# A pad of 96 or 224 bytes at the left end of the on-chip memory, in a two-layer decoder trunk

## The chip, the cores and the metric

The kernel runs on one core of one Trainium2 chip. The metric is the device time of one execution in microseconds; lower is better. Before the change the median of three runs is 2179.43 us (2175.47 to 2182.7).

## The reference

The program is a decoder trunk with 1024 positions, width 1024 and two layers, all in float32. Layer 0 mixes tokens with latent attention (12 heads, causal), layer 1 with sliding-window attention (12 query heads, window 128). In both layers 4 more heads attend to a memory of 256 rows. A layer ends in an output projection and a squared-ReLU MLP of width 4096:

```python
for i in range(DEPTH):
    hn = rmsnorm(x, attn_norm_g[i])
    mix, q_cross = mla_mixer(hn, ...) if i % 2 == 0 else swa_mixer(hn, ...)
    cross = memory_cross_attention(q_cross, mem_n, w_mem_kv[i])
    x = x + jnp.concatenate([mix, cross], axis=-1) @ w_o[i]
    a = jax.nn.relu(rmsnorm(x, mlp_norm_g[i]) @ w_up[i])
    x = x + (a * a) @ w_down[i]
return rmsnorm(x, final_norm_g)
```

## The kernel before, in words

**Matmuls in three parts.** Every large operand is split into a high part (rounded to the matmul type float32r) and a low part, the rest. A product is then three matmuls: high times high, high times low, low times high. Each is a stationary operand of 128x128, loaded by a weight load, against a moving operand of 128x512. In the rows of the profile the moving operand stands first behind the arrow: `psu<-x,d` writes the accumulator `psu`, streams `x`, and has `d` loaded as weights.

**The MLP.** Both big products use Strassen's scheme with seven block products, in two stages. The *up* stage takes 16 steps of 256 columns, each with seven products of 4 x 3 = 12 matmuls (lines 1347 to 1349, accumulators psu and psv). The *down* stage takes 7 x 16 steps, each of 4 x 3 matmuls (lines 1638 to 1640, psy and psz).

```python
1346            for k in range(4):
1347                nc.tensor.matmul(ps, wh[:, k, :], xh[:, k, :], ...)
1348                nc.tensor.matmul(ps, wh[:, k, :], xl[:, k, :], ...)
1349                nc.tensor.matmul(ps, wl[:, k, :], xh[:, k, :], ...)
```

In the up stage ACT multiplies the incoming weights by the gain (line 1247), DVE sums them, and ACT and DVE split them (lines 99 and 100) four products ahead of the matmuls; the DMAs of the raw weights are issued two steps ahead, into `mr` for even steps and into `d` for odd ones. What the chip does first and next is the order of the code: each engine has one list, and the DMAs named here are issued by SP.

**Other stages with large matmuls.** The output projection (`wo_phase`, lines 108 to 110, accumulator pswo) goes over its columns in two halves; the first half reads its weights from `woq`, the second from `g`. The input projection of layer 1 (`feat_mm`, lines 108 to 110, accumulator psf) makes 12 blocks of 128 features, each 2 x 24 matmuls; the first 6 blocks have their weights in `wsh` and `wsl`, the last 6 in `wf`. The input projection of layer 0 is psin (lines 117 to 120). Attention has the accumulators pss, psx, pso (layer 0), psw and a second pswo of 384 columns (layer 1) and pscx (memory).

**Two stacks of tiles.** On-chip memory is 128 partitions; a tile has the same byte address in each. Pools are stacked from both ends: `side="left"` from the low end, `"right"` from the high end. At the low end lies the pool `const`, whose last tile is the pad `padl`; above it lies `quad`, and then whichever left pool the stage needs. At the high end lies the pad `padr`, and then the right pools. The pads are filled with zeros once and read by nobody.

```python
220    padl = const.tile([P, 24], F32, name="padl")
221    padr_p = pool("padr", "right")
222    padr = padr_p.tile([P, 24], F32, name="padr")
223    nc.gpsimd.memset(padl, 0.0)
```

Nearly all large tiles are whole multiples of 512 bytes in a row (a row of 512 columns is 2048 bytes, a weight slice of 128 columns is 512), so all slices in a pool begin at one and the same place within 512 bytes. The addresses in the built program give these places:

| pools | side | tiles as the profile names them | place within 512, before |
|---|---|---|---|
| quad | left | mqq, mqf, mr, xnh, woq, wf, fa, xhls | 256 |
| hb, kvp, kv1p, qcp, q1p | left | q and k of every third head of layer 0, v, kh and kl, q, qc, kmh and kml of layer 1 | 256 |
| pa | left | wih, wil (rows of 3712 bytes) | 256, 128, 0, 384 in turn |
| rest, xnp, ws (the MLP's and wo_phase's) | right | d, i, g; x; uh, ul, wsh, wsl | 384 |
| hb1, at | right | the other heads, ph, pl, vh | 384 |
| cp, wu | right | cTh, cTl, wkv, wkn, wqr | 128 |

`quad` begins at byte 19,200, which is 37 x 512 + 256. So a matmul that takes one operand from quad and the other from a right pool has them at two places that differ by 128 bytes; one with both operands on one side mostly has them at equal places. The matmuls of 512 columns of the first kind are: four of the seven products of every up step (mqq and mqf move, i, x and d are loaded), the first half of both output projections (woq), most of psf, and 96 matmuls at the end of layer 1's down stage (`psy<-mqq,x`).

Of the kernel before, what the change touches and what calls it, by code (L numbers as in the profile page):

```python
# [9 lines left out]
F32 = mybir.dt.float32  # L10
# [9 lines left out]
P = 128  # L20
# [35 lines left out]
def trunk(  # L56
# [12 lines left out]
    def pool(name, side="left", space=None, bufs=1):  # L69
        kw = {"reuse_waits": "tile"}  # L70
        if space is not None:
            kw["space"] = space
        return tc.alloc_tile_pool(name=name, bufs=bufs, side=side, **kw)

    const = pool("const")
# [141 lines left out]
    cosb = const.tile([P, NT, 16], F32, name="cosb")  # L217
    sinb = const.tile([P, NT, 16], F32, name="sinb")

    padl = const.tile([P, 24], F32, name="padl")  # L220
    padr_p = pool("padr", "right")
    padr = padr_p.tile([P, 24], F32, name="padr")
    nc.gpsimd.memset(padl, 0.0)
# [1756 lines left out]
```

## Time and profile before

| | |
|---|---|
| median of three runs | 2179.43 us |
| profiled execution: span from first to last instruction | 2179.5 us |
| TensorE matmul busy | 2133.9 us, 98% of the span, 10045 instructions |
| VectorE, ScalarE, GpSimd busy | 1489.4, 1149.7, 162.7 us |
| mean granted TensorE clock | 0.991 |

Consecutive matmuls overlap in the records: the next starts some 230 ns after one whose recorded time is some 390 ns. What a matmul costs in a dense stretch is therefore the distance from its start to the start of the next, which the timeline shows. A row of groups reads: line, engine, operation, output<-moving,weights, shape, count | busy us, mean ns of one | idle us before it. A row of windows reads: from:to, length, busy us (count) of PE, of PEld (weight loads), of DVE, ACT and POOL, then the granted clock, the busy share of the DMA engines and GB/s. A row of waits reads: who waited, for whom: us in total, times, longest us. A row of the chain reads: start us, us, what.

### The profile page before, as it was taken

Reading aid. Unit: us, or ns where it says so; the run is one execution under the profiler, and the core shown is the slowest. Engines: PE = TensorE matmul, PEld = TensorE weight load, DVE = VectorE, ACT = ScalarE, POOL = GpSimd, SP = SyncE. Lnnn points to the kernel's source line nnn. Section 1 sums busy time; section 2 is a strip of 40 time slices with the busy share of each in tenths; the row PEclk is TensorE's granted clock in tenths of the full one; section 3 lists DMA queues with packets and bytes.
Section 4 is the critical chain, followed back from the end, with each engine's and each line's share of the span. In section 5 each row is a group of like instructions: output and inputs, shape, how many; then the busy total and the mean of one; then the engine's idle time right before and its main releaser. Section 6 shows DMA issues by size and latency. Waiting matters only on the chain.

```text
span 2179.5 us, 29333 instructions
## 1 busy us (share of the span) xinstructions
PE 2133.9 (98%) x10045; PEld 1719.3 (79%) x10045; DVE 1489.4 (68%) x2845; ACT 1149.7 (53%) x2494; POOL 162.7 (7%) x226
## 2 busy tenths in 40 slices
PE   7999999999999999999999999999999999999998
PEld 6888677668788888788888778668888888888887
DVE  7566678765887776786657453665887776885665
ACT  5455477765754444444445453776755544444452
POOL 0012000001000000000001133440000000000000
PEclk9999999989999999999999999999999999999999
DMA  7202222323254445964533111113254445954442
GB/s 249 66 1 67 51 59 46 88 92 110 80 175 151 144 144 170 341 197 126 165 117 107 53 39 49 39 55 120 78 179 145 160 157 177 329 183 145 127 120 88
DMA packets 170948, 271.96 MB, mean 125 GB/s; under 512 B 15681, under 2 KB 71726, under 8 KB 170798
## 3 DMA queue, kind: packets, MB, share of 16 engines
q1 hardware_dynamic: 164228, 253.80, 36.3%
q0 software_dynamic: 4016, 13.12, 1.7%
q10 hardware_dynamic: 2554, 3.17, 0.4%
q8 instruction: 79, 1.29, 0.2%
q14 instruction: 71, 0.58, 0.1%
HBM read 180.65 MB, written 76.81 MB: 118 GB/s over the span
## 4 chain that ended last, share of the span: by engine, by line
PE 89%; DVE 4%; ACT 3%; DMA 2%; issue 1%; POOL 0%; DVEq 0%; ACTq 0%; POOLq 0%
PE psy L1640 5%; PE psy L1638 5%; PE psy L1639 5%; PE psu L1349 5%; PE psu L1347 5%; PE psu L1348 5%; PE pss L850 4%; PE psz L1640 4%; PE psz L1638 4%; PE psz L1639 4%; PE psv L1349 4%; PE psv L1348 4%; PE psv L1347 4%; PE pso L880 3%; PE pswo L110 3%; PE pswo L108 2%
## 5 line engine op out<-in xcount | busy, mean ns | idle before, releaser
L1247 ACT ACTIVATE mr<-mr,gcol 128x256 f32<-128x256 f32 (+1 forms) x160 | 67.4, 477 | 63.8 <-DMA mr<-in_mlp_w_up_dram 56.8
L1638 PE MATMUL psy<-g 128*128 128x512 f32 x256 | 99.9, 390 | 0.0
L1639 PE MATMUL psy<-g 128*128 128x512 f32 x256 | 99.6, 389 | 0.0
L1640 PE MATMUL psy<-g 128*128 128x512 f32 x256 | 99.4, 390 | 0.0
L99 ACT ACTIVATE g<-i 128x512 fp32r<-128x512 f32 x79 | 49.7, 629 | 93.3 <-PE psz L1639 46.2
L860 ACT ACTIVATE p<-pss 128x384 f32<-128x384 f32 (+3 forms) x144 | 69.5, 486 | 55.1 <-PE pss L850 51.7
L99 ACT ACTIVATE i<-mr 128x512 fp32r<-128x512 f32 x78 | 49.1, 630 | 84.9 <-PE psu L1348 21.7
L1247 ACT ACTIVATE d<-d,gcol 128x256 f32<-128x256 f32 x128 | 57.9, 499 | 62.0 <-DMA d<-in_mlp_w_up_dram 55.2
L100 DVE TENSOR_TENSOR g<-i,g 128x512 fp32r<-128x512 f32 x79 | 55.1, 698 | 47.0 <-ACT g L99 47.0
L99 ACT ACTIVATE uh<-i 128x512 fp32r<-128x512 f32 x66 | 41.6, 630 | 84.6 <-PE psy L1639 40.7
L731 DVE TENSOR_REDUCE m<-psx 128x1 f32<-128x1024 f32 (+7 forms) x96 | 71.9, 752 | 16.4 <-PE psx L730 16.0
L100 DVE TENSOR_TENSOR pl<-p,ph 128x512 fp32r<-128x512 f32 (+3 forms) x120 | 62.0, 526 | 30.4 <-ACT ph L99 29.1
L100 DVE TENSOR_TENSOR uh<-i,uh 128x512 fp32r<-128x512 f32 x66 | 45.5, 689 | 43.1 <-ACT uh L99 43.1
L1638 PE MATMUL psz<-g 128*128 128x512 f32 x192 | 74.7, 389 | 0.0
L1639 PE MATMUL psz<-g 128*128 128x512 f32 x192 | 74.7, 389 | 0.0
L1640 PE MATMUL psz<-g 128*128 128x512 f32 x192 | 74.7, 389 | 0.0
L100 DVE TENSOR_TENSOR i<-mr,i 128x512 fp32r<-128x512 f32 x78 | 53.6, 687 | 22.4 <-ACT i L99 22.4
L850 PE MATMUL pss<-ql,kh 97*128 97x384 f32 (+3 forms) x144 | 64.7, 449 | 0.0
L99 ACT ACTIVATE ph<-p 128x512 fp32r<-128x512 f32 (+3 forms) x120 | 59.5, 501 | 2.9
L1563 DVE TENSOR_TENSOR mqf<-mqq,mqf 128x512 f32<-128x512 f32 x64 | 43.1, 687 | 25.1 <-DMA mqq<-in_mlp_w_down_dram 24.9
L1640 PEld LDWEIGHTS psy<-g 128*128 128x128 f32 x256 | 48.0, 188 | 10.0
L1639 PEld LDWEIGHTS psy<-g 128*128 128x128 f32 x256 | 48.1, 188 | 9.9
(633 smaller groups left out, 7035.6 us busy)
## 6 DMA issues: line engine op xcount, KB each, us to landing
i<-hd SPq DMA_DIRECT2D x154, 256.0 KB
hd<-uh SPq DMA_DIRECT2D x76, 256.0 KB
hd<-ul SPq DMA_DIRECT2D x76, 256.0 KB
mr<-in_mlp_w_up_dram SPq DMA_DIRECT2D x36, 512.0 KB
hd<-x SPq DMA_DIRECT2D x72, 256.0 KB
mr<-hd SPq DMA_DIRECT2D x70, 256.0 KB
d<-in_mlp_w_up_dram SPq DMA_DIRECT2D x32, 512.0 KB
mqq<-in_mlp_w_down_dram SPq DMA_DIRECT2D x32, 512.0 KB
```

What stands on the lines that cost most here:

```text
L99: nc.scalar.activation(hi, src, AF.Copy)
L100: nc.vector.tensor_tensor(lo, src, f32(hi), ALU.subtract)
L731: return lambda: nc.vector.reduce_max(m8s[h][:, i : i + 1], ps[:, :n], axis=AX, negate=True)
L850: return lambda: nc.tensor.matmul(o, a, b, skip_group_check=True, **kw)
L860: nc.scalar.activation(p[:, c0:], ps, AF.Exp, scale=SC)
L1247: nc.scalar.activation(w[:, k, :], w[:, k, :], AF.Copy, scale=g_mlp[layer][:, k0 + k : k0 + k + 1])
L1347: nc.tensor.matmul(ps, wh[:, k, :], xh[:, k, :], start=p in (1, 2, 5) and k == 0, stop=False, skip_group_check=True)
L1348: nc.tensor.matmul(ps, wh[:, k, :], xl[:, k, :], start=False, stop=False, skip_group_check=True)
L1349: nc.tensor.matmul(ps, wl[:, k, :], xh[:, k, :], start=False, stop=k == 3, skip_group_check=True)
L1638: nc.tensor.matmul(ps, ah[:, j, :], bh, start=p in (1, 5, 2) and k == 0, stop=False, skip_group_check=True)
L1639: nc.tensor.matmul(ps, ah[:, j, :], bl, start=False, stop=False, skip_group_check=True)
L1640: nc.tensor.matmul(ps, al[:, j, :], bh, start=False, stop=k == NP - 1, skip_group_check=True)
```

## The change

One number changes:

```diff
-    padl = const.tile([P, 24], F32, name="padl")
+    padl = const.tile([P, 56], F32, name="padl")
```

The pad takes 224 bytes where it took 96. Every left tile above it moves up by 128 bytes: quad from 19,200 to 19,328, which is 37 x 512 + 384. The places within 512 become 384 for quad, hb, kvp, kv1p, qcp and q1p, and 384, 256, 128, 0 in turn for pa. The other tiles of const and all right tiles stay where they were.

The lists of instructions of PE, DVE, ACT and SP are the same before and after. On POOL one row differs, at the start of the program, where the pads are filled (`ident` is the identity, `eps_t` a constant):

```order
 L124 MEMSET ident 128x128
 L138 MEMSET eps_t 128x1
-L223 MEMSET padl 128x24
+L223 MEMSET padl 128x56
 L224 MEMSET padr 128x24
 L143 DMA sinks_b<-in_swa_sinks_dram 128x12
```

Nothing moved: the filling of the pad has 32 columns more, and what follows stands in the same order.

## The prediction

> **What bounds the kernel now.** I read the page first, for its busy shares and the chain that ended last.
>
> ```profile
> span 2179.5 us, 29333 instructions
> PE 2133.9 (98%) x10045; PEld 1719.3 (79%) x10045; DVE 1489.4 (68%) x2845; ACT 1149.7 (53%) x2494; POOL 162.7 (7%) x226
> PE 89%; DVE 4%; ACT 3%; DMA 2%; issue 1%; POOL 0%; DVEq 0%; ACTq 0%; POOLq 0%
> ```
>
> The chain runs through PE for 89% of the span. Since a recorded matmul overlaps the next one, a busy PE may still be slow, so the windows by stage come next: the first half of layer 0's output projection, its up stage, one up step, a piece of its down stage, the wf blocks of layer 1's input projection, and layer 1's up stage.
>
> ```profile
> 485.00:530.00 45.00, 44.34 (x192) 35.30 (x191) 30.12 (x41) 27.10 (x60) 3.85 (x7) 1.00 0.47 156
> 606.00:894.00 288.00, 287.99 (x1250) 234.21 (x1250) 208.34 (x328) 138.70 (x279) 1.90 (x1) 1.00 0.51 171
> 642.62:661.99 19.37, 19.37 (x86) 15.77 (x84) 14.14 (x23) 9.51 (x19) 0.00 (x0) 1.00 0.44 146
> 950.00:1050.00 100.00, 100.00 (x442) 82.78 (x442) 67.52 (x109) 42.69 (x74) 0.00 (x0) 1.00 0.47 145
> 1309.00:1375.00 66.00, 66.00 (x285) 53.12 (x284) 23.43 (x31) 21.31 (x32) 18.02 (x41) 1.00 0.14 41
> 1575.00:1866.00 291.00, 291.00 (x1264) 237.08 (x1263) 214.75 (x340) 142.18 (x284) 0.00 (x0) 1.00 0.51 171
> ```
>
> In the up and wf stages PE has no idle time at all, with the clock granted in full (1.00). So their time is the number of matmuls times the distance between two starts, and anything that shortens that distance is worth all of it. In one up step of 19.37 us DVE is busy for 14.14 and ACT for 9.51 us; neither becomes the bound if the step shrinks by a third of a microsecond.
>
> Is the distance the same for all matmuls? The groups by form say no. First the four kinds of product in the up stage and one of the down stage, all 128x512 with the same three-part scheme:
>
> ```profile
> L1348 PE MATMUL psv<-mqq,i 128*128 128x512 f32 x112 | 44.2, 395 | 0.0
> L1348 PE MATMUL psv<-mqf,x 128*128 128x512 f32 x112 | 44.2, 395 | 0.0
> L1348 PE MATMUL psv<-g,d 128*128 128x512 f32 x112 | 43.6, 389 | 0.0
> L1348 PE MATMUL psu<-x,d 128*128 128x512 f32 x128 | 49.8, 389 | 0.0
> L1639 PE MATMUL psy<-g 128*128 128x512 f32 x256 | 99.6, 389 | 0.0
> ```
>
> The two that stream a quad tile (place 256) against right weights (place 384) take 395 ns, the three with both operands at 384 take 389. They alternate within one step of 19 us, beside the same work of the other engines. The timeline of PE in the step from 642.62 gives the distance: 48 matmuls of the first kind up to 653.81, then 36 of the second up to the next step.
>
> ```profile
> 642.62 0.40 PE L1347 MATMUL psu<-mqq,i 128*128 128x512 f32 x1
> ...
> 653.81 0.39 PE L1347 MATMUL psu<-g,i 128*128 128x512 f32 x1
> ...
> 661.99 0.40 PE L1347 MATMUL psu<-mqq,i 128*128 128x512 f32 x1
> ```
>
> That is 11.19 / 48 = 233.1 ns each, against 8.18 / 36 = 227.2 ns. A longer stretch of equal places, 78 distances in the down stage, fixes the pace that I expect after the change:
>
> ```profile
> 1000.14 0.39 PE L1638 MATMUL psy<-g 128*128 128x512 f32 x1
> ...
> 1017.82 0.39 PE L1638 MATMUL psy<-g 128*128 128x512 f32 x1
> ```
>
> 17.68 / 78 = 226.7 ns.
>
> **The change part by part.** The longer filling of the pad is one POOL instruction ahead of the first matmul's inputs, 32 columns more; POOL is busy 7% of the span and the chain gives it 0%: nothing. All the rest is places: quad moves from 256 to 384, where the right tiles are.
>
> *Up stages.* 48 of the 84 matmuls of a step go from 11.19 us to 48 x 226.7 ns = 10.88 us: 0.31 us a step. 16 steps in two layers: 32 x 0.31 = 9.9 us. By the recorded durations (395 against 389) it is 1536 x 6 ns = 9.2 us; I take 9.9, since the distance is what adds up.
>
> *Output projections.* The first halves read weights from woq, the second halves from g:
>
> ```profile
> L109 PE MATMUL pswo<-woq,x 128*128 128x512 f32 x64 | 25.3, 395 | 0.0
> L109 PE MATMUL pswo<-woq,d 128*128 128x512 f32 x64 | 25.3, 395 | 0.0
> L109 PE MATMUL pswo<-g,d 128*128 128x512 f32 x112 | 43.6, 390 | 0.0
> ```
>
> Each of the two upper rows is one of three lines in one layer: 2 x 192 = 384 matmuls at 5 ns, 1.9 us. Here PE does idle a little (44.34 busy of 45.00 us), so between 0 and 1.9; I take 1.9, because PE is busy for 98% of that window.
>
> *Input projection of layer 1, wf blocks.* Both xnh and wf are in quad, x is on the right, so one matmul in three has unequal places; yet all three are slow:
>
> ```profile
> L108 PE MATMUL psf<-xnh,wf 128*128 128x512 f32 x96 | 38.1, 397 | 0.0
> L109 PE MATMUL psf<-x,wf 128*128 128x512 f32 x96 | 37.9, 395 | 0.0
> L110 PE MATMUL psf<-xnh,wf 128*128 128x512 f32 x96 | 37.7, 392 | 0.0
> 1310.10 0.40 PE L108 MATMUL psf<-xnh,wf 128*128 128x512 f32 x1
> ...
> 1312.20 0.40 PE L108 MATMUL psf<-xnh,wf 128*128 128x512 f32 x1
> ```
>
> Nine distances take 2.10 us, 233.3 ns each. After the change all three kinds are at 384, which is the state of the down stage: 288 x (233.3 - 226.7) = 1.9 us. That a matmul at equal places pays here for its neighbours means the price belongs to the stream, not to one pair.
>
> *The wsh blocks.* Weights on the right, two of three moving operands in quad. Fifteen distances:
>
> ```profile
> 1300.00 0.39 PE L109 MATMUL psf<-x,wsh 128*128 128x512 f32 x1
> ...
> 1303.43 0.39 PE L109 MATMUL psf<-x,wsh 128*128 128x512 f32 x1
> ```
>
> 3.43 / 15 = 228.7 ns: 288 x 2.0 = 0.6 us.
>
> *End of layer 1.* 96 matmuls with xnh's old tiles:
>
> ```profile
> L1639 PE MATMUL psy<-mqq,x 128*128 128x512 f32 x32 | 12.6, 395 | 0.0
> ```
>
> 96 x 6 = 0.6 us.
>
> *Layer 0's input projection and attention.* wih's rows go round through all four places against weights in quad; both shift alike, so their relative places stay, and I take 0. If the absolute place counted, 192 matmuls could gain 5 ns (1.0 us):
>
> ```profile
> L118 PE MATMUL psin<-wil,xhls 128*128 128x512 f32 x64 | 25.2, 394 | 0.0
> ```
>
> Attention has its operands at equal places on one side already: 0.
>
> *DMAs into left tiles.* These now end at places that are odd multiples of 128, as the right ones always did. The up weights land in both kinds of tile in turn, mr on the left, d on the right:
>
> ```profile
> ACT mr L1247 <- DMA mr<-in_mlp_w_up_dram: 56.8, 27, 3.1
> ACT d L1247 <- DMA d<-in_mlp_w_up_dram: 55.2, 24, 3.4
> ```
>
> A wait is 56.8 / 27 = 2.1 us for the left and 55.2 / 24 = 2.3 us for the right, 9% more at most. In the up stage PE covers that. It isn't covered where the chain itself stands on a load into a left tile:
>
> ```profile
> 37.07 4.88 DMA fa<-in_mla_w_in_dram
> 44.29 3.23 DMA fa<-in_mla_w_in_dram
> 430.61 3.96 DMA wor<-in_w_o_dram
> 886.71 7.64 DMA mqf<-in_mlp_w_down_dram
> ```
>
> These are 19.71 us; 9% is 1.8 us. Between 0 and 1.8 I take half, +0.9. The Trainium skill ("DMA: Bandwidth & Descriptors", How a descriptor splits into AXI transactions) speaks against the change here: a transaction must start at a multiple of 256 bytes, so a piece that starts elsewhere costs an extra, partly unused one. By it a 1 KB piece would need 36 beats for 32, an estimate of 12.5% or 2.5 us in place of 0.9; the trace's 9% in waits neither excludes it nor needs it.
>
> Sum: 9.9 + 1.9 + 1.9 + 0.6 + 0.6 = 14.9 us gained, less 0.9: 14.0. The profiled execution has a span of 2179.5 us, the median of the runs is 2179.43, so no correction: 2179.5 - 14.0 = **2165.5 us**, 0.64% less.
>
> **The rivals.** A change of over 0.3% (6.5 us) is what a measurement of this kernel can tell from none.
>
> *The left side is slow wherever its tiles begin: 2179.5 us.* Every slow row above has a quad operand, so side and place are confounded in the MLP. Two rows part them, a matmul of 256 columns with both operands on the left at 256, and one of 384 with both on the right at 128:
>
> ```profile
> L379 PE MATMUL pscx<-kml,qc 128*128 128x256 f32 x64 | 15.9, 282 | 0.0
> L120 PE MATMUL psv<-wkvh,cTl 128*128 128x384 f32 x32 | 8.5, 335 | 0.0
> ```
>
> On the right, 128 columns fewer cost 389 - 335 = 54 ns less, so 256 columns should take 335 - 54 = 281. The left takes 282. A left side that is slow by itself would have added some 3 to 6 ns. The wf rows keep this rival alive: there even left with left is slow. Chance 0.10. The Trainium skill ("TensorE: Matmul & The Clock Gate", Part 2, on the weight load) would have it so too: the moving operand and the weight load have two independent read ports, and a load takes no bandwidth from the running matmul. By that rule places could not matter; the alternation of 395 and 389 within a step is not explained by it.
>
> *Only part of it goes: about 2172.5 us.* If a part of the price hangs on something else that tells quad from the rest, half of the 14.0 us comes. Nothing in the rows gives a half, except that wsh blocks with two unequal pairs in three pay only 2.0 ns. Chance 0.05.
>
> *Equal places collide on the left: 2183.9 us.* The slowest row of all, 397 ns, is a pair with both operands in quad at the same place. If that is what equal places do as soon as a quad tile is in the pair, the 1536 + 384 + 192 + 96 = 2208 matmuls of the terms above (192 of the wsh blocks) go from 395 to 397: 2208 x 2 ns = 4.4 us more. It decides if the up products come out above 395. Against it: the same line's sister, L110, has equal places too and takes 392, and all right-right rows stand at 389. Chance 0.03.
>
> **How the numbers follow.** My forecast has 0.82. By itself it reaches from 2179.5 - 14.9 - 1.0 = 2163.6 (no DMA price, psin gains) to 2179.5 - 14.9 + 1.9 + 1.8 = 2168.3 (no gain in the output projections, the whole DMA price). The runs shown lie from 4.0 below to 3.3 above their median, and the forecast stands on one execution, so I add that and a little for terms that I took at 0 (4.6 below, 5.7 above): 2159 to 2174. That holds the forecast and most of the half case, and leaves out under 2 in 10. Faster by over 0.3%: nearly all of the forecast and half of the half case, 0.84. Within 0.3%: the first rival, the rest of the half case, part of the collision, 0.13. Slower by more: 0.03, the collision with the DMA price on top.
>
> **What would show it.** Right: the rows psu and psv <- mqq and mqf fall from 395 to 389 and an up step from 19.37 to 19.05 us; the three wf rows become one number near 389; the rows of g and of attention stand still; in the up windows PE stays at 100%. The DMA term is right if waits for mr come near those for d. Wrong: mqq and mqf rows still at 395 (the side, not the place), between 390 and 394 (part of it), above 395 (a collision); or the rows fall and the span doesn't, in which case PE idles in the up windows and ACT or a DMA is what it waits for.

## The result

| | median us | runs | against the kernel before |
|---|---|---|---|
| before | 2180.88 | 13 (2175.47 to 2183.93) | |
| changed | 2174.58 | 13 (2171.13 to 2179.19) | 0.9973, 95% interval 0.9963 to 0.9983 |

The change is worth 6.3 us, 0.27%. The forecast was 14.0 us. So the kernel is faster, by less than half of what was expected.

### The profile page after: what moved, and what is told of

Same layout as the page of the kernel before. It is cut to its first block, busy times and chain, and to the rows that moved or that the text cites. A ratio compares the mean times of both kernels' runs of the same rounds, so it can differ in the third digit from the quotient of the medians.

```text
span 2169.4 us, 29333 instructions
## 1 busy us (share of the span) xinstructions
PE 2118.5 (98%) x10045; PEld 1714.9 (79%) x10045; DVE 1488.9 (69%) x2845; ACT 1147.7 (53%) x2494; POOL 161.2 (7%) x226
## 3 DMA queue, kind: packets, MB, share of 16 engines
q1 hardware_dynamic: 164228, 253.80, 37.2%
## 4 chain that ended last, share of the span: by engine, by line
PE 84%; DVE 5%; DMA 4%; ACT 4%; issue 1%; POOL 0%; SPq 0%; DVEq 0%; ACTq 0%; POOLq 0%
PE psy L1638 5%; PE psy L1640 5%; PE psy L1639 5%; PE psu L1347 4%; PE psu L1349 4%; PE psu L1348 4%; PE psz L1638 4%; PE psz L1640 4%; PE psz L1639 4%; PE pss L850 4%; PE pso L880 3%; PE psv L1349 3%; PE psv L1348 3%; PE psv L1347 3%; PE pswo L110 2%; PE pswo L108 2%
```

## The profile after

The page of the changed kernel first: its span, its engines and the chain that ended last.

```profile
span 2169.4 us, 29333 instructions
PE 2118.5 (98%) x10045; PEld 1714.9 (79%) x10045; DVE 1488.9 (69%) x2845; ACT 1147.7 (53%) x2494; POOL 161.2 (7%) x226
PE 84%; DVE 5%; DMA 4%; ACT 4%; issue 1%; POOL 0%; SPq 0%; DVEq 0%; ACTq 0%; POOLq 0%
```

PE is busy for 15.4 us less (2133.9 before), of which some 5.5 us aren't the pad's work, as shown below. The chain stands on PE for 84% instead of 89%; DMA and ACT have grown in it. The groups by form after, the row of product 7 first:

```profile
L1347 PE MATMUL psu<-g,i 128*128 128x512 f32 x120 | 48.9, 408 | 3.6 <-ACT d L1386 2.0 <-ACT i L1386 1.4
L1348 PE MATMUL psv<-mqq,i 128*128 128x512 f32 x112 | 43.6, 389 | 0.0
L1348 PE MATMUL psv<-mqf,x 128*128 128x512 f32 x112 | 43.6, 389 | 0.0
L1348 PE MATMUL psv<-g,d 128*128 128x512 f32 x112 | 43.6, 389 | 0.0
L108 PE MATMUL psf<-xnh,wf 128*128 128x512 f32 x96 | 37.3, 389 | 0.0
L109 PE MATMUL psf<-x,wf 128*128 128x512 f32 x96 | 37.3, 389 | 0.0
L110 PE MATMUL psf<-xnh,wf 128*128 128x512 f32 x96 | 37.3, 389 | 0.0
L109 PE MATMUL pswo<-woq,x 128*128 128x512 f32 x64 | 24.9, 390 | 0.0
```

Before, the first of them was:

```profile
L1347 PE MATMUL psu<-g,i 128*128 128x512 f32 x120 | 47.0, 391 | 0.0
```

The slow rows shown have come down to 389 or 390 (395 before for mqq, mqf and woq; 397, 395 and 392 for wf), and the row of g with d stands still. The rows of wsh and wsl have not (405, 397 and 397 ns after, 407, 396 and 398 before), although their distances became a little shorter. The timeline of PE in the step that the prediction looked at (it began at 642.62 before) gives the distances:

```profile
635.18 0.39 PE L1347 MATMUL psu<-mqq,i 128*128 128x512 f32 x1
...
646.06 0.39 PE L1347 MATMUL psu<-g,i 128*128 128x512 f32 x1
...
654.22 0.39 PE L1347 MATMUL psu<-mqq,i 128*128 128x512 f32 x1
```

10.88 us for 48 matmuls and 8.16 for 36: 226.7 ns each in both, 19.04 us for the step (19.37 before). So far this is the forecast, to a hundredth of a microsecond. What is new is the first line of product 7, with 408 ns and 3.6 us of idle time (before: 391 and none). The windows show where it goes: the two up windows of the prediction, moved to the same matmuls, and inside the first the step above and the next one (second and third row).

```profile
598.55:887.25 288.70, 285.55 (x1251) 233.65 (x1251) 209.23 (x330) 138.31 (x279) 1.90 (x1) 1.00 0.51 170
635.18:654.22 19.04, 19.04 (x85) 15.77 (x84) 13.99 (x23) 9.37 (x19) 0.00 (x0) 1.00 0.46 149
654.22:674.17 19.95, 19.34 (x85) 15.69 (x84) 13.95 (x23) 9.33 (x19) 0.00 (x0) 1.00 0.41 135
1565.50:1855.20 289.70, 289.19 (x1265) 236.22 (x1264) 212.70 (x339) 140.97 (x284) 0.00 (x0) 1.00 0.52 171
```

The first step is as forecast. The next takes 19.95 us, more than the 19.37 of before, with PE idle for 0.61. The whole window takes 288.70 us where it took 288.00, and that of layer 1 took 291.00 and now 289.70: nearly all of the 9.9 us that the matmuls should save in the up stages is handed back there.

The timeline of the late step, PE first, shows one matmul that starts 1.00 us after the one before it:

```profile
664.88 0.39 PE L1349 MATMUL psv<-mqf,x 128*128 128x512 f32 x1
665.88 0.50 PE L1347 MATMUL psu<-g,i 128*128 128x512 f32 x1 [0.61 <-ACT d L1386]
```

It is the first of product 7. Products 6 and 7 both write `psu`, so product 7 must wait until ACT has copied product 6 out of it (line 1386). ACT in the same microseconds:

```profile
659.64 0.63 ACT L99 ACTIVATE i<-d 128x512 fp32r<-128x512 f32 x1 [1.03 <-PE psv L1348]
663.92 0.91 ACT L1247 ACTIVATE mr<-mr,gcol 128x256 f32<-128x256 f32 x2 [3.65 <-DMA mr<-in_mlp_w_up_dram]
664.73 0.61 ACT L99 ACTIVATE x<-d 128x512 fp32r<-128x512 f32 x1
665.25 0.57 ACT L1386 ACTIVATE d<-psu 128x512 f32<-128x512 f32 x1
```

ACT stood still for 3.65 us, waiting for the second half of a later step's raw weights; the gain of that half (line 1247) stands on ACT's list ahead of the copy that PE needs. The same place before the change:

```profile
671.00 0.91 ACT L1247 ACTIVATE mr<-mr,gcol 128x256 f32<-128x256 f32 x2 [2.82 <-DMA mr<-in_mlp_w_up_dram]
671.81 0.62 ACT L99 ACTIVATE x<-d 128x512 fp32r<-128x512 f32 x1
672.34 0.57 ACT L1386 ACTIVATE d<-psu 128x512 f32<-128x512 f32 x1
```

The same order, the same wait, but the copy ended at 672.91 and product 7 started at 673.22: some 0.3 us to spare in this step. After, product 7 is due 0.31 us earlier in the step, and the copy ends 0.68 us later in it (11.60 us after the step's start, 10.92 before). The load took most of that: from its issue to the start of its gain there are 5.27 us, and 4.66 before. The list of waits after:

```profile
ACT mr L1247 <- DMA mr<-in_mlp_w_up_dram: 75.1, 31, 3.8
ACT d L1247 <- DMA d<-in_mlp_w_up_dram: 67.9, 23, 4.2
...
PE psu L1347 <- ACT d L1386: 2.0, 3, 1.1
```

ACT waits for weights 143.0 us where it waited 112.0. The idle time that PE records is only part of the loss (0.61 us at the step above, where the start came 0.77 late). Summed over all distances between starts in the up stages that are longer than 300 ns, less 227 ns for each, PE loses 9.0 us after and 1.2 before: 7.8 more. Product 7 has 7.5 of the 9.0, and 0.3 of the 1.2.

The step shown is not like all others. From the end of the copy to the start of product 7, the 28 steps that follow the first two of each layer had between 0.05 and 1.94 us before, most of those of layer 1 0.9 to 1.2. After, 16 of the 28 have 0.05, which means that PE starts as soon as the copy is done. So the copies lost more than the 0.31 us by which product 7 came earlier, and the traces show two things that go with it:

- The second half is issued later in PE's step: 4.2 us after the step's start before and 4.9 after (means of ten steps of layer 1; 4.5 and 4.9 in layer 0).
- Four steps of layer 0 (4, 7, 10 and 13, counted from 0) lose 4.2 of the 7.5 us. In these the last packet of the load landed 3.9 to 4.7 us after the issue, where the median of all second halves is 3.5 to 3.6. In each of the four a packet of 16 KB ran beside the load for 1.05 to 1.57 us, on the queue that the profile names `instruction`; 9 to 27 of the load's 512 packets landed later than 3.6 us, the others did not. Before, steps 4, 7 and 10 have such a packet too, of 0.9 to 1.0 us, and landings of 3.9 to 4.2 us; in step 13 it came when the load had all but landed. That this packet is the cause was not tested. The row of that queue, with its packets, its MB and their share of the 16 engines' time:

```profile
q8 instruction: 79, 1.29, 0.3%
```

The two profiled executions differ by 10.1 us, the medians by 6.3. Part of that is the granted clock: in the attention of layer 0 it was 0.50 for 13.65 us before.

```profile
462.26:475.91 13.65, 13.65 (x32) 7.63 (x31) 3.86 (x7) 4.18 (x9) 0.00 (x0) 0.50 0.05 10
```

After the change the same stretch ran at full clock:

```profile
461.70:469.80 8.10, 8.10 (x34) 4.66 (x33) 3.76 (x6) 4.79 (x10) 0.00 (x0) 1.00 0.00 0
```

These 13.65 - 8.10 = 5.5 us are no work of the pad. The other way, a stretch at 0.50 in the attention of layer 1 was 3.4 us longer after (6.83 against 3.41), where PE lost 1.4 us.

## The experiments

The theory: the matmuls bring the 14.9 us of the prediction's sum everywhere, and some 8 of them are handed back in the up stages, because ACT's copy of product 6 is late behind a gain that waits for a DMA. The rivals: DMAs into left tiles are slower at their new place (A); something else than the weights is late (B). Since the up stages hold the whole question, this table has for every kernel the time from the first matmul of step 2 to the first of step 15, for both layers together (26 steps, read from the timelines of PE), and the long distances as counted above. Each interval is against runs of the kernel before that were taken beside it, whose medians were 2180.4 to 2181.3 us. By the prediction the 26 steps should go from 503.8 to 503.8 - 26 x 0.31 = 495.7 us.

| kernel | places left, right | median us | ratio to before, 95% interval | 26 up steps, us | long distances, us |
|---|---|---|---|---|---|
| before | 256, 384 | 2180.9 | | 503.8 | 1.2 |
| changed | 384, 384 | 2174.6 | 0.9963 to 0.9983 | 503.6 | 9.0 |
| changed, loads by POOL | 384, 384 | 2188.4 | 1.0020 to 1.0049 | 520.1 | 26.1 |
| before, loads by POOL | 256, 384 | 2191.3 | 1.0029 to 1.0061 | 518.3 | 17.2 |
| both at 256 | 256, 256 | 2168.9 | 0.9925 to 0.9964 | 499.0 | 4.4 |
| left at 320 | 320, 384 | 2184.6 | 1.0002 to 1.0025 | 506.3 | 3.3 |
| changed, copy by DVE | 384, 384 | 2164.8 | 0.9921 to 0.9957 | 495.9 | 3.3 |
| before, copy by DVE | 256, 384 | 2179.1 | 0.9982 to 1.0011 | 503.6 | 1.1 |
| changed, writes by POOL | 384, 384 | 2170.0 | 0.9941 to 0.9977 | 498.7 | 5.0 |
| both at 256, copy by DVE | 256, 256 | 2165.4 | 0.9923 to 0.9955 | 495.3 | 2.2 |
| both at 320 | 320, 320 | 2173.4 | 0.9956 to 0.9983 | 504.4 | 9.9 |
| 256 apart | 192, 448 | 2175.0 | 0.9968 to 0.9988 | 504.2 | 10.4 |

### Earlier loads, a failed attempt

```diff
-                nc.sync.dma_start(out=r[h], in_=...)
+                (nc.gpsimd if h and i > 2 else nc.sync).dma_start(out=r[h], in_=...)
```

On the changed kernel:

> The changed kernel, with the loads of the second half of each step's up weights (from step 3 on) issued by POOL instead of SP, so that they no longer stand behind SP's writes of the last results. Theory: the shorter distance (226.7 instead of 233.3 ns) is worth some 15 us on PE everywhere, and the up stages hand back 7.8 us because PE at product 7 (psu<-g,i) waits for ACT's evacuation of product 6, which is queued on ACT behind the gain of a half that has not landed. With the loads some 1.5 us earlier the wait at product 7 goes (under 2 us in place of 5.6 in the rows L1386), and the time is 2174.6 - 7 = about 2167. Rival A, loads into left tiles are slower at their new place: the waits of ACT's gain for mr stay longer than in the kernel before, and of the 7.8 us little comes back, 2172 to 2175. Rival B, something else than the weights (DVE's sums, the evacuations themselves) is late: PE's idle time at product 7 stays, 2174 to 2176.

And on the kernel before:

> The same edit of the loads on the kernel before (pad of 96 bytes), the control for the run above. Theory: PE had no idle time in the up stages of the kernel before, its step being 0.3 us longer, so earlier loads are worth at most 1.2 us there: 2179.5 to 2181. The pad is then worth 13 to 14 us between this pair, against 6.3 without the edit. Rivals A and B: the edit is worth as much or as little with either pad, so the pair stays 6 to 7 us apart.

Measured: 2188.4 and 2191.3 us. Both expectations fell, because the edit did the reverse of what it was chosen for. The list of DMA issues of the first of the two gives, for the loads that POOL issued:

```profile
d<-in_mlp_w_up_dram POOLq DMA_DIRECT2D x14, 512.0 KB, 5.2
mr<-in_mlp_w_up_dram POOLq DMA_DIRECT2D x12, 512.0 KB, 5.2
```

SP's issues have no such number in the list. Counted alike, from the issue of a second half to the start of its gain where ACT waited for it, the medians are 5.2 us when POOL issues and 4.0 when SP does (kernels before and after). So the pair is a test with later weights. As such it speaks for the theory: PE's wait at product 7 grows

```profile
L1347 PE MATMUL psu<-g,i 128*128 128x512 f32 x120 | 49.9, 416 | 16.5 <-ACT d L1386 8.3 <-ACT i L1386 8.1
```

from 3.6 to 16.5 us, still behind ACT's line 1386, and with both kernels waiting for weights the pad is worth only 2.9 us.

### Product 6's copy by DVE: the deciding run

```diff
-                nc.scalar.activation(s, ps, AF.Copy)
+                V.tensor_copy(s, ps) if p == 6 and i > 1 else nc.scalar.activation(s, ps, AF.Copy)
```

> The changed kernel, with product 6's copy out of its accumulator made by DVE instead of ACT from step 2 on (28 copies of 128x512), so that it no longer stands on ACT's list behind the gain that waits for the weights; loads, places and PE's list stay. Theory: PE's wait at product 7 for this copy (9.0 us of long distances in the up stages, 1.2 in the kernel before) falls to 3 us or less, and the time is 2174.6 - 6 = about 2168.5 (2167 to 2171). The loads still land as late as before (ACT still waits some 140 us for them), so a gain here shows that it is the place of the copy on ACT's list that costs, not the load by itself. Rival B, DVE is late as well (it is busy 14 of 19 us of a step): the wait at product 7 becomes one for DVE of the same size, 2173 to 2176. Rival E, the weights themselves are late for product 2 or 6 of the next step: PE's idle time moves there, 2173 to 2176.

Its control, with the pad of before:

> The same edit on the kernel before (pad of 96 bytes), the control of the run above. Theory: there is hardly anything to take away (1.2 us of long distances), and DVE has 28 copies more to do: 2179.5 to 2182. The pad is then worth 12 to 14 us between this pair, nearly the 14.9 of the matmuls. If the edit helps by as much here as there, the copy on ACT's list is a cost of its own and not what the pad's gain ran into: 2174 to 2176.

Measured: 2164.8 and 2179.1 us. The same edit is worth 9.8 us with the long pad, and 1.4 with the short one against the runs beside it (2180.5), where the interval holds no change. Between this pair the pad is worth 14.3 us by the medians. The rows of the changed kernel with this edit, groups and waits:

```profile
L1347 PE MATMUL psu<-g,i 128*128 128x512 f32 x120 | 46.7, 389 | 0.0
```

```profile
ACT mr L1247 <- DMA mr<-in_mlp_w_up_dram: 71.3, 31, 3.6
ACT d L1247 <- DMA d<-in_mlp_w_up_dram: 59.5, 23, 4.3
```

Product 7 doesn't wait any more (the 3.3 us of long distances that are left stand elsewhere, the largest, 1.0 us, in the last step of layer 1), although ACT still waits for weights for 130.8 us. So the late landing costs nothing by itself; what costs is that the copy stands behind it. The second halves are issued 4.3 us after the step's start in layer 1 here, as early as before the change, though the step is as short as in the changed kernel. So the later issue (4.9 us) came with the wait and not from the shorter step; through which link is not shown. The windows over the 26 steps:

```profile
621.84:869.52 247.68, 247.68 (x1092) 205.12 (x1093) 192.16 (x301) 112.28 (x226) 1.90 (x1) 1.00 0.49 161
1586.67:1834.93 248.26, 247.99 (x1094) 204.84 (x1093) 193.48 (x304) 113.45 (x227) 0.00 (x0) 1.00 0.49 162
```

247.68 / 13 = 19.05 us a step in layer 0, the number of the prediction, and 19.10 in layer 1. Rival B falls: DVE has the copies in addition (192.16 us busy of 247.68) and PE doesn't wait for it there. Rival E falls too: in the 26 steps only 0.7 us of long distances are left. The time came out 4 us below the expected 2168.5; the edit took away the whole wait and not two thirds of it. The 26 steps account for 7.7 of the 9.8 us; the rest is within the intervals. The nearer edit, the copy ahead of the gain on ACT's own list, was not run.

### Both sides at 256

```diff
     padl = const.tile([P, 24], F32, name="padl")
...
-    padr = padr_p.tile([P, 24], F32, name="padr")
+    padr = padr_p.tile([P, 56], F32, name="padr")
```

> The kernel before with the left pad as it was (96 bytes) and the right pad 128 bytes longer: both sides now have their large tiles at place 256, equal as in the change, and at a multiple of 256 bytes, which the changed kernel's are not. Theory: equality is what counts, not which place: rows of psu and psv<-mqq and mqf at 389 ns, wf rows in one, the same idle time at product 7 as in the changed kernel (5 to 6 us), and the time of the changed kernel within 2 us: 2172.5 to 2176.5. Rival A, the place of a DMA's end counts: all loads of the up stage land earlier than in either kernel (means of 3.0 to 3.3 us from issue to landing for 3.5 to 3.7), the idle time at product 7 falls, and the time is 2166 to 2170. Rival C, place 384 is the quick one by itself: all rows at 395, 2184 or more.

Measured: 2168.9 us, inside the range of rival A, and its rows of the groups show the matmuls of the theory:

```profile
L1347 PE MATMUL psu<-g,i 128*128 128x512 f32 x120 | 48.2, 401 | 1.2 <-ACT i L1386 0.9 <-ACT d L1386 0.2
L1348 PE MATMUL psv<-mqq,i 128*128 128x512 f32 x112 | 43.6, 389 | 0.0
L1348 PE MATMUL psv<-mqf,x 128*128 128x512 f32 x112 | 43.6, 389 | 0.0
```

So equality is what the matmuls ask for, and rival C falls. The time is lower than the theory gave, and PE waits less at product 7 (1.2 us idle in place of 3.6, 3.1 us of long distances there in place of 7.5). Whether the place of the loads does that, as rival A has it, is not shown. The landing times of 3.0 to 3.3 us that it named did not come: the median is 3.5 us here and 3.5 to 3.6 in the kernels before and after, and the median packet of 1 KB on SP's queue took 46 ns in all three. From the issue of a second half to the start of its gain, right tiles `d` take 4.02 us here and 4.26 in the changed kernel, left tiles `mr` 4.07 and 4.21 (means of 12 and 10 loads from step 5 on for which ACT waited), but the medians are 3.90 and 4.05, 3.93 and 3.96, and ACT's waits for weights add up to 142.2 us here and 143.0 there. Of the 4.4 us that product 7 loses less, 1.4 are in a single step, step 13 of layer 0: the packet on the instruction queue came 3.4 us after the load's issue here and 1.3 us after it in the changed kernel.

Is it this wait through which both sides at 256 gain 5.7 us? If so, the place is worth nothing once the copy is made by DVE:

> Both sides at place 256 (right pad longer, left pad as it was), and product 6's copy by DVE. Theory: both savings are of the same wait (4.35 us of long distances remain with both sides at 256), so together they give the full 14.9 us of the matmuls and little more: 2165 to 2168, against 2168.9 with both at 256 alone. If the gain of place 256 over 384 (5.7 us) were not the wait at product 7 but something else that adds to it, this run would come out at 2161 to 2164.

Measured: 2165.4 us (0.9939, as the same edit with both sides at 384). So the gain goes through that wait, as far as five runs of each kernel can tell.

### SP's list freed of the writes

```diff
-            nc.sync.dma_start(out=hd[p][i * P : (i + 1) * P, :], in_=a)
+            (nc.gpsimd if 1 < i < NP - 2 else nc.sync).dma_start(out=hd[p][i * P : (i + 1) * P, :], in_=a)
```

In the changed kernel SP issued the load of the example at 658.65, right behind a write of a result that DVE had just made:

```profile
658.24 0.32 SPq L1381 DMA_DIRECT2D hd<-ul  x1
658.65 0.39 SPq L1270 DMA_DIRECT2D mr<-in_mlp_w_up_dram  x1
```

> The changed kernel, with the writes of the up stage's results (hd, steps 2 to 13) issued by POOL instead of SP: SP's list is then free for the loads of the weights, which stay on SP's own queue (3.5 to 3.7 us from issue to landing, where the loads issued by POOL took 5.2). Theory: the loads of the second half are issued when their tile is free, some 1 us earlier, ACT waits less for them and PE's wait at product 7 falls from 9.0 to 2 to 4 us: 2167 to 2171. Rival F, the loads are late because the DMA queues are full and not because SP is: landing times grow by as much as the issue is earlier, 2173 to 2176. POOL's writes take longer to be issued and read DVE's tiles later, so the ring of results (12 tiles) could be held up; PE would then wait for DVE at line 1391 or 1399: over 2176.

Measured: 2170.0 us, in the theory's range, with nearly half of the long distances gone (5.0 us are left, 3.0 of them at product 7, where 2 to 4 were expected). Rival F has its part: the second halves are issued 2.1 us earlier in the step (2.8 us after its start in place of 4.9) and now take 4.7 to 4.8 us from issue to landing (medians; 3.5 to 3.6 in the changed kernel), so 1.2 us of the earlier issue are lost; ACT's waits, 53.1 and 47.1 us, still fell to 100.2. How late the weights are is thus partly a matter of SP's list.

### How far apart, and in what unit

One pad 64 bytes longer than before:

```diff
-    padl = const.tile([P, 24], F32, name="padl")
+    padl = const.tile([P, 40], F32, name="padl")
```

> The kernel before with a left pad of 160 bytes: left tiles at place 320, 64 bytes from the right ones at 384. It asks whether the price of unequal places depends on the distance. Theory, any inequality costs the same: rows of mqq and mqf at 395 ns, no idle time at product 7, the time of the kernel before (2179 to 2182). Rival D, what counts is a coarser place (within 128 bytes or so the two are equal), or a price that grows with the distance: rows at 389 to 392 and 2174 to 2178. Left with left and right with right stay at 389 in each case.

The row of the groups:

```profile
L1348 PE MATMUL psu<-mqq,i 128*128 128x512 f32 x112 | 44.1, 394 | 0.0
```

64 bytes apart cost as much as 128: 394 ns and 233 ns from start to start. The theory's expectation holds for the rows, and rival D falls. At 2184.6 us the kernel is 3.2 us slower than before in the runs beside it (2181.3), and 2.6 above the range: the long distances are 2.1 us more, and the wsh blocks, whose distances were 226 to 233 ns by line, have 230 to 237.

Both pads 64 bytes longer (`padl` and `padr` 40 columns):

> Both pads 64 bytes longer than before (160 bytes each): left and right tiles all at place 320, equal but at a multiple of 64 only. Theory, equality is what the matmuls ask for: rows of mqq and mqf at 389 ns, distances near 227 ns, as with both sides at 256 or 384; the wait at product 7 depends on how late the weights land at 320, so between the 2168.9 of both at 256 and the 2174.6 of both at 384, 2168 to 2176. Rival G, the place itself counts too and 320 is a bad one: all large matmuls at 392 ns or more, on the right as well, and 2184 or more.

Measured: 2173.4 us, rows of mqq, mqf and wf at 389, distances 227. Any equal place serves the matmuls. Rival G falls. The wait at product 7 is as in the changed kernel (9.9 us of long distances): of the three equal places 256 alone has a shorter one.

Both pads 64 bytes shorter (8 columns each):

> Both pads 64 bytes shorter than before on the left and on the right (32 bytes each): left tiles at place 192, right ones at 448, 256 bytes apart. Theory, any inequality within 512 bytes costs the same: rows of mqq and mqf at 394 to 396 ns, distances of 232 to 234 ns, and 2179 to 2186, as with 64 and 128 bytes apart. Rival H, the price repeats every 256 bytes (a 256-byte row or line is the unit): rows at 389 ns and the time of the changed kernel, 2168 to 2176. Rival I, the price grows with the distance: rows above 400 ns and more than 2190.

The rows of the groups:

```profile
L1348 PE MATMUL psu<-mqq,i 128*128 128x512 f32 x112 | 43.6, 389 | 0.0
L108 PE MATMUL psf<-xnh,wf 128*128 128x512 f32 x96 | 37.3, 389 | 0.0
```

Rival H, against the theory: 256 bytes apart cost nothing. The rows, the distances (226.6 to 227.1 ns) and the time (2175.0 us) are those of equal places. So the place that counts, in the pairs tried, is the one within 256 bytes, not within 512 as the change and the prediction put it. It made no difference to the forecast, since the two are 128 apart in both counts.

## Why the prediction was right and wrong

**What bounds the kernel; the distance between starts.** Right, and shown: some 227 ns in all the matmuls of the sum that had stood 128 bytes apart.

**Up stages, 9.9 us.** The term was right for the matmuls and wrong for the span. The step that failed: "In the up and wf stages PE has no idle time at all [...] So their time is the number of matmuls times the distance between two starts, and anything that shortens that distance is worth all of it." No idle time says that nothing was late before; it does not say how much there was to spare. "In one up step of 19.37 us DVE is busy for 14.14 and ACT for 9.51 us; neither becomes the bound" compared busy times. ACT was free for half of the step and late all the same, since it stood in a wait with PE's copy behind it: 2.82 us in the step after the one quoted, where the copy had 0.3 us to spare. The row of that wait (ACT for mr, 56.8 us) was quoted in the prediction, and was used for the DMA's price alone. In the 26 steps the change brought 0.2 us of the 8.1; with the copy made by DVE in both kernels it brings 7.7 (503.6 to 495.9). Measured, the term of 9.9 was about 2: it saved 9.9 on the matmuls and lost 7.8 to the wait. The time, 2174.6, is 0.6 us above the range.

**Output projections and wf blocks, 1.9 each; end of layer 1, 0.6.** Right by the rows: woq and wf stand at 389 to 392 (down from 395 to 397 in the slowest), and the wf blocks come out 0.32 us a block earlier (6 x 0.32 = 1.9).

**wsh blocks, 0.6.** Smaller, about 0.3: their distances went from 226 to 233 ns by line to 227 to 228.

**DMAs into left tiles, +0.9; "In the up stage PE covers that."** Wrong in the same way: the cover was thin. The 9% came from waits, which hold the slack of other engines too, and not from transfers. On the chain itself the loads named (19.71 us before) took 19.86 us after, so next to nothing there (a fifth one stands on the chain now, at the same place of layer 1):

```profile
35.65 4.72 DMA fa<-in_mla_w_in_dram
44.82 3.92 DMA fa<-in_mla_w_in_dram
431.06 3.81 DMA wor<-in_w_o_dram
879.96 7.41 DMA mqf<-in_mlp_w_down_dram
1847.91 7.70 DMA mqf<-in_mlp_w_down_dram
```

In the up stages the three kernels with equal matmuls off 256 lost 9.0 to 10.4 us in long distances and the one with both sides at 256 4.4; that the loads' place made this difference is not shown. The Trainium skill ("DMA: Bandwidth & Descriptors", How a descriptor splits into AXI transactions) gives a start off a multiple of 256 bytes an extra transaction, worded there for reads; the estimate of 12.5% from it was not seen. It would be 6 ns on a packet of 1 KB, and the median one of SP's queue took 46 ns before, after, with both sides at 256 and with both at 320. All packets of that queue took 37.2% of 2169.4 us = 807 us after and 36.2% of 2163.9 us = 783 us with both sides at 256, but 36.7% of 2168.5 us = 796 us at the same places as after with the copy by DVE, so about half of these 3% is no matter of place.

**The rivals.** The left side is not slow by itself (the rows of mqq, mqf and wf are at 389), and equal places do not collide. The half that came, 6.3 us, looks like the rival "only part of it goes", but its reason is another: all of the price went, and half of it was given back. That its 2172.5 us lie near the 2174.6 measured is chance. What the prediction named as its last sign of an error, rows that fall and a span that doesn't, with PE idle in the up windows and ACT as what it waits for, is what happened.

**The sum.** 14.9 - 7.8 = 7.1 us against 6.3 measured (3.7 to 8.1 by the interval).

The Trainium skill ("TensorE: Matmul & The Clock Gate", Part 2, on the weight load) has the moving operand and the load read by independent ports, so that a load takes no read bandwidth from the running matmul. By that the places could not matter, and in the runs they do: with the two sides 64 or 128 bytes apart within 256 a matmul took 6 ns more than with both at equal places. Why it does is not shown.

A version that beats both kernels came out of it: the changed kernel with product 6's copy by DVE, 2164.8 us (0.9939, 0.9921 to 0.9957).

## What to carry to other kernels

A stage in which the bounding engine never idles tells nothing about how near the next engine is: before counting a saving in full, read for each thing that engine waits for how much earlier than needed it is done, and look on that helper's list for a wait that stands ahead of it. Here a copy with 0.05 to 1.9 us to spare took nearly the whole saving of the up stages, on an engine that was busy for half of the time, and once it was late the loads behind it were issued later too. When a helper is late by its order and not by its work, moving one short instruction can be worth more than hurrying the transfer: 9.8 us for the copy, 4.5 for the earlier loads.

## What the runs showed of the hardware

- In the MLP's 128x512 float32r matmuls, each with a weight load of its own, one starts some 227 ns after the one before it when moving operands and weights begin at the same place within 256 bytes (384 and 384, 256 and 256, 320 and 320, 192 and 448), and about 233 ns after it when the two sides are 64 or 128 bytes apart.
- In the wf blocks before, one matmul in three had unequal places, and all three were slow: distances of 236, 234 and 230 ns by line, and 226 to 227 after.
- At 128 apart the distances are of two kinds (229 to 232 and 237 to 238 ns in the rows of mqf before), at 64 apart all are 233 or 234; the means agree.
- Loads of 512 KB issued by POOL reached ACT 5.2 us after their issue (median), where the same loads issued by SP took 4.0, and the edit cost the changed kernel 14 us (2174.6 to 2188.4).
- A load of 512 packets that shared its time with a 16 KB packet of the instruction queue (1.05 to 1.57 us) landed 3.9 to 4.7 us after its issue, where the median is 3.5 to 3.6, by 9 to 27 late packets (four loads of layer 0 in the changed kernel; with both sides at 320 the same four took 4.0 to 4.7). That the one delays the other is not tested.
- The median packet of 1 KB took 46 ns whether the tile began at 256, 320 or 384 within 512 bytes. A kernel that moves only the loaded tiles wasn't made.
